# Load order and slots of the expert weights, load order and ends of the modulation slabs in a two-layer decoder trunk

## The chip, the cores and the metric

The kernel runs on one core of one Trainium2 chip, in one launch. The metric is the device time in microseconds (us): the median of the timed runs. Besides them there is one profiled execution, from which every row below is read.

## The reference

One sequence of 512 tokens with 1024 features, float32, goes through two layers. Each layer is a mixer and then a mixture of experts; both are modulated by a vector `c` through `mod = silu(c) @ ada_w + ada_b`, six groups of 1024 columns for each layer.

```python
for layer in range(2):
    sh1, sc1, g1, sh2, sc2, g2 = split(silu(c) @ ada_w[layer] + ada_b[layer], 6)
    h = x * (1 + sc1) + sh1
    y = moba_gla_mixer(h) if layer == 0 else gated_deltanet_mixer(h)
    x = layer_norm(ALPHA * x + g1 * y)
    h = x * (1 + sc2) + sh2
    # every token: 6 of 64 experts, each silu(h @ gate) * (h @ up) @ down, 1024 -> 256 -> 1024, and one shared expert
    x = layer_norm(ALPHA * x + g2 * moe_ffn(h))
```

All weights are float32 and are read once. One expert has three matrices of 1 MiB (gate, up, down); two layers of 64 experts are 384 MiB of the 572 MB that the core moves.

## The kernel before

**The expert loop** (`moe`). The experts are ordered by how many tokens chose them and packed into 38 blocks (`BLOCKS`): 20 blocks hold one expert, 14 hold two and 4 hold four (blocks 8, 16, 26 and 34), so that a block has at most 128 rows of tokens. Iteration b issues on TensorE, whose order is written out by hand here (`manual_schedule`): the down matmuls of block b-1 (`narrow`, L1369), the gate and up matmuls of block b (`widen`, L1336), sums of finished blocks into the residual (`combine`, L1396), transposes of the next block's tokens (`turn`, L1324) and of the hidden values (`turn_back`, L1347). Where block b-1 has one expert, `widen` goes first. A block of four runs its `narrow` in two halves of two experts; the `widen` of the next block stands between them.

**Where weights land.** Gate and up of an expert go into one of five wide buffers in turn (`eslot`: two `w2`, two `parts`, one `wx`). Down goes into a ring of three buffers (`slot`, tag `w`, `NRING`), which all other weight slabs use too. A buffer is taken in turn, so a load waits until the matmuls that read its buffer's last content are over.

**Order of the loads** (`loads`, `fetch`). All weight loads are issued by SyncE's queue (SP), in the order in which the generator `loads` makes them. It alternates one expert's gate and up (`weight_in`) with the down (`weight_out`) of the expert three places earlier (`LAG = 3`). At the end the last three downs go into wide buffers. `fetch` says how far the generator has come when iteration b is written: all loads of blocks up to b + 2, and two more.

**The modulation slabs.** `ada_slabs` makes nine items for each group of 2048 columns: eight loads of 1 MiB, each followed by one multiply-accumulate on VectorE into one buffer `acc` (L254, L256), and an end. The end (`mod_end`, L268, L269) turns `acc` with sixteen TensorE transposes and sums it with four VectorE reductions. Group (0, 0) is done first, in `start`: its end makes `hT`, the modulated and turned input. The other five groups are spread over layer 0: `fill` runs about three items at each weight slab of the mixer and of `out_project`. When the next item is an end and it isn't the first of its call, `fill` stops and leaves it for the next call. After `out_project` a loop runs what is left. Outside the loop of experts the order on each engine is a planner's, by the order of the program and its own costs.

**Around the start.** `start` loads seven slabs, then the first weight slab of the mixer (`first`), then the eighth slab. The end of the group computes, for each of eight k, `hT[0]` on ScalarE (L1749) and, on VectorE, the product in place (L1750) and the remainder `hT[1]` (L1751). `split` (L218, L220) makes the high and low part of a weight slab on ScalarE and VectorE (or GpSimd, L225) into one of two `parts` buffers.

Of the kernel before, what the change touches and what calls it, by code (L numbers as in the profile page):

```python
# [10 lines left out]
F32 = mybir.dt.float32  # L11
# [4 lines left out]
OP = mybir.AluOpType  # L16
PSUM = bass.MemoryType.PSUM

P = 128
D = 1024  # L20
KT = 8
# [5 lines left out]
FE = 256  # L27
# [6 lines left out]
NX = 1  # L34
EARLY = 4
LEAD = 3
LAG = 3
FOLD = 2
LANES = 64
ALPHA = float(4 ** 0.25)  # L40
# [93 lines left out]
class Kernel:  # L134
# [1181 lines left out]
    def turn(self, M, G):  # L1316

        nc = self.nc
        xT = G["xT"] = M["pool"].tile([P, KT, P], F32, tag="xT", name="xT", bufs=2)
        xv = G["xg"].rearrange("p (c k) -> p k c", k=KT)  # L1320
        for g in range(2):
            pt = self.ptile("tr")
            for k in range(4):
                nc.tensor.transpose(pt[:, k * P:(k + 1) * P], xv[:, 4 * g + k, :], self.ident)  # L1324
            nc.scalar.activation(xT[:, 4 * g:4 * g + 4], pt.rearrange("p (k c) -> p k c", k=4), AF.Copy)  # L1325

    def widen(self, M, G):

        nc, xT = self.nc, G["xT"]
        pg = self.ptile("mm")  # L1330
        pv = pg.rearrange("p (j c) -> p j c", j=2)
        h = G["h"] = M["pool"].tile([P, FE], F32, tag="hh", name="hh", bufs=2)
        for g in range(0, len(G["w"]), 2):
            for i in range(KT):
                for a, n, w in G["w"][g:g + 2]:
                    nc.tensor.matmul(pv[a:a + n], xT[:, i, a:a + n], w[0][:, :, i], start=(i == 0), stop=(i == KT - 1))  # L1336
        nc.scalar.activation(h, pg[:, :FE], AF.Silu)  # L1337
        nc.vector.scalar_tensor_tensor(h, h, G["wt"], pg[:, FE:], op0=OP.mult, op1=OP.mult)  # L1338
        yield
# [59 lines left out]
    def eslot(self, M):  # L1399

        k = M["w"] = (M.get("w", -1) + 1) % (NW2 + 2 + NX)
        if k < NW2:
            return self.tab.tile([P, 4096], F32, tag="w2", name="wslot2", bufs=NW2)
        if k < NW2 + 2:
            return self.parts().rearrange("p j c -> p (j c)").bitcast(F32)
        return M["pool"].tile([P, 4096], F32, tag="wx", name="wslot3", bufs=NX)

    def shared(self, hT, wp, ws):

# [61 lines left out]
    def moe(self, l, hT, nxt, pre=None):  # L1471
# [31 lines left out]

        def loads():

            last = []
            for k, b in enumerate(BLOCKS):
                es = [i if i < SINGLE else nc.values_load(
                    M["order"][:, i:i + 1], engines=SPE, min_val=0, max_val=E - 1,
                    skip_runtime_bounds_check_because="the places are a permutation of the experts") for i, _, _ in b]  # L1510
                w = [[] for _ in es]
                W.append([(a, n, x) for (_, a, n), x in zip(b, w)])
                for x, e in zip(w, es):
                    x.append(self.weight_in(l, e, self.eslot(M)))
                    yield
                    last.append((x, e))
                    while len(last) > (0 if k < SINGLE else LAG):
                        x, e = last.pop(0)
                        x.append(self.weight_out(l, e, self.slot()))
                        yield  # L1520
            for x, e in last:
                x.append(self.weight_out(l, e, self.eslot(M)[:, :2048]))
                yield

        load, started, total = loads(), [0], 2 * E

        def fetch(n):

            while started[0] < min(n, total):
                next(load)  # L1530
                started[0] += 1
# [21 lines left out]
        with ExitStack() as es:  # L1553
# [13 lines left out]
            with self.tc.manual_schedule(engines={mybir.EngineType.PE}):  # L1567
                fetch(sum(2 * len(x) for x in BLOCKS[:LEAD]) + 2)
                self.turn(M, G[0])
                for b in range(NB + 1):  # L1570
# [6 lines left out]
                            todo.append(G[b - 1])  # L1577
                    if b < NB:
                        fetch(sum(2 * len(x) for x in BLOCKS[:b + LEAD]) + 2)
                        G[b]["w"], G[b]["one"] = W[b], len(W[b]) == 1  # L1580
                        row.append(self.widen(M, G[b]))
                    if not todo:
# [131 lines left out]
    def start(self, hT, t4):  # L1714
# [20 lines left out]
        def end(acc):  # L1735
            av = acc.rearrange("p (m c k) -> p m k c", m=2, k=KT)
            for g in range(4):
# [9 lines left out]
                for k in range(2 * g, 2 * g + 2):  # L1747
                    x = xT[k // 2][:, k % 2]
                    nc.scalar.activation(hT[0][:, k], x, AF.Identity, scale=md[:, 1, k:k + 1], bias=md[:, 0, k:k + 1])  # L1749
                    nc.vector.tensor_scalar(x, x, md[:, 1, k:k + 1], md[:, 0, k:k + 1], op0=OP.mult, op1=OP.add)  # L1750
                    nc.vector.tensor_sub(hT[1][:, k], x, hT[0][:, k].bitcast(F32))  # L1751

        spare = []
# [8 lines left out]
            return spare.pop()  # L1762

        todo = self.ada_slabs(0, 0, t4, end, slot)
        for f in todo[:-2]:
            f()
        w_in = d["ev_w_in"][0]
        first = self.slab(w_in, 2048, 256)
        todo[-2]()
        todo[-1]()  # L1770
        self.first = {2048: self.split(first)}
        self.first[3072] = self.split(self.slab(w_in, 3072, 16))
# [1 line left out]
    def run(self):  # L1774
# [5 lines left out]
        with ExitStack() as es:  # L1780
# [8 lines left out]
            def fill(n=3):  # L1789

                n, left[0] = n + left[0], 0
                for i in range(n):
                    if not queue:
                        if not todo:
                            return
                        l, g = todo.pop(0)
                        queue.extend(self.ada_slabs(l, g, t4, self.mod_end(l, g)))
                    if i and len(queue) == 1:
                        left[0] = n - i
                        return  # L1800
                    queue.pop(0)()
# [96 lines left out]
```

## Time and profile before

| | us |
|---|---|
| Median of 3 runs (2145.56 to 2153.2) | 2150.31 |
| Profiled execution, its own time | 2150.13 |
| Span of its instructions | 2148.1 |

| Stretch (us from the start of the span) | What runs |
|---|---|
| 0 to 40.4 | group (0, 0) of the modulation, turning of the input |
| 40.4 to 280.3 | mixer of layer 0 |
| 280.3 to 350 | `out_project` of layer 0 |
| 350 to 402.5 | input of the experts, routing, shared expert |
| 402.5 to 1028 | expert loop of layer 0, first to last expert matmul |
| 1389.6 to 1446.1 | `out_project` of layer 1 |
| 1496.2 to 2117.1 | expert loop of layer 1 |

The engines are PE (TensorE), PEld (its weight loads), DVE (VectorE), ACT (ScalarE), POOL (GpSimd) and SP (SyncE). A small letter q after an engine is its sequencer. An arrow in brackets at the end of a row tells for how long the engine was idle before it and what ended that. PEclk is the granted TensorE clock: 1.00 is 2.4 GHz, 0.50 is 1.2 GHz.

### The profile page before, as it was taken

The page shows a single profiled execution, that of the slowest core. Times are in us where ns is not written, and L with a number is a line of the kernel's source. Part 1 is how long each engine was busy: PE and PEld are TensorE (multiplying, and loading weights), DVE is VectorE, ACT ScalarE, POOL GpSimd, SP SyncE. Part 2 cuts the span into 40 slices and gives each one's busy share as a digit, 9 for nine tenths or more (in the row PEclk, how much of TensorE's full clock was granted, in tenths as well). Part 3 has the DMA queues.
Part 4 walks back from the last instruction along what each step waited for, and adds up shares of the span by engine and source line. Part 5 has one row for each costly group of instructions (what it writes and reads, how often), then busy time and mean ns, then how long its engine had stood idle before and what let it go on. Part 6 is the DMA issues. An engine that isn't in the chain of part 4 may idle for free. (4 is left out here: it accounts for less than half of the span.)

```text
span 2148.1 us, 28655 instructions
## 1 busy us (share of the span) xinstructions
PE 1955.6 (91%) x10619; PEld 1193.5 (56%) x10619; DVE 1236.2 (58%) x3169; ACT 508.3 (24%) x969; POOL 441.2 (21%) x313
## 2 busy tenths in 40 slices
PE   4999878999999999999688999999999999998995
PEld 3777778644443443443567877888443444443432
DVE  6666687844444553542778778578453535544436
ACT  3412533111111111111334455523111111111110
POOL 1222234111010110101034445144211010110102
PEclk9999998999999999999899999999999999999997
DMA  7765455998998989988332111128989989989893
GB/s 296 257 240 186 182 199 195 352 330 325 406 349 351 389 316 361 381 325 300 96 118 59 40 60 60 46 99 309 357 335 365 363 327 402 353 317 405 329 348 126
DMA packets 128679, 572.18 MB, mean 266 GB/s; under 512 B 16943, under 2 KB 54255, under 8 KB 72473
## 3 DMA queue, kind: packets, MB, share of 16 engines
q1 hardware_dynamic: 103600, 499.81, 60.1%
q0 software_dynamic: 19632, 55.79, 9.3%
q10 hardware_dynamic: 5304, 14.72, 1.9%
q8 instruction: 85, 1.39, 0.3%
q14 instruction: 58, 0.47, 0.1%
HBM read 550.33 MB, written 34.61 MB: 272 GB/s over the span
## 5 line engine op out<-in xcount | busy, mean ns | idle before, releaser
L1336 PE MATMUL ps_mm<-wslot,xT 128*64 128x512 f32 (+2 forms) x1216 | 404.5, 596 | 1.1 <-ACT xT L1325 0.8
L1369 PE MATMUL ps_mm<-wslot,hT 128*64 128x512 f32 (+2 forms) x1024 | 329.6, 627 | 20.1 <-DMA wslot<-in_moe_w_down_dram 19.9
L1338 DVE SCALAR_TENSOR_TENSOR hh<-hh,t,ps_mm 128x256 f32<-128x256 f32 x76 | 36.5, 480 | 434.5 <-ACT hh L1337 434.5
L1336 PE MATMUL ps_mm<-parts,xT 128*64 128x512 f32 (+2 forms) x832 | 280.0, 595 | 0.7 <-ACT xT L1325 0.4
L1336 PEld LDWEIGHTS ps_mm<-wslot,xT 128*64 128x64 f32 (+2 forms) x1216 | 142.1, 148 | 218.9 <-issue 205.7
L1369 PEld LDWEIGHTS ps_mm<-wslot,hT 128*64 128x64 f32 (+2 forms) x1024 | 105.5, 152 | 225.1 <-issue 197.5
L232 PE MATMUL ps_mm<-parts,hTh 128*128 128x256 f32 x704 | 206.7, 295 | 14.0 <-DVE op L400 6.9
L1294 POOL DMA_INDIRECT xg<-hd,idx x76 | 86.3, 1136 | 615.1 <-PE ps_tr L1396 525.4
L233 PE MATMUL ps_mm<-parts,hTh 128*128 128x256 f32 x704 | 204.0, 291 | 4.9 <-DVE parts L220 4.2
L234 PE MATMUL ps_mm<-parts,hTl 128*128 128x256 f32 x704 | 203.3, 291 | 0.0
L225 POOL TENSOR_TENSOR parts<-wslot,parts 128x512 fp32r<-128x512 f32 (+1 forms) x79 | 140.6, 1807 | 241.9 <-ACT parts L218 241.8
L1397 DVE TENSOR_TENSOR x<-x,ps_tr 128x512 f32<-128x512 f32 x288 | 183.6, 680 | 11.1 <-PE ps_tr L1396 10.4
L1337 ACT ACTIVATE hh<-ps_mm 128x256 f32<-128x256 f32 x76 | 29.2, 384 | 613.7 <-PE ps_mm L1336 613.7
L1376 POOL DMA_INDIRECT acc<-yh,row x40 | 64.8, 1620 | 498.9 <-DVE yh L1375 498.9
L1336 PEld LDWEIGHTS ps_mm<-parts,xT 128*64 128x64 f32 (+2 forms) x832 | 93.7, 144 | 130.5 <-issue 122.9
L1396 PE MATMUL ps_tr<-yh,ohs 128*128 128x512 f32 x288 | 137.4, 477 | 26.1 <-DVEq L1690 14.0
L232 PEld LDWEIGHTS ps_mm<-parts,hTh 128*128 128x128 f32 x704 | 137.3, 195 | 17.7 <-DVE op L400 4.6
L1325 ACT ACTIVATE xT<-ps_tr 128x512 f32<-128x512 f32 x152 | 84.0, 597 | 245.0 <-PE ps_tr L1324 245.0
L233 PEld LDWEIGHTS ps_mm<-parts,hTh 128*128 128x128 f32 x704 | 137.4, 195 | 6.8 <-DVE parts L220 4.8
L234 PEld LDWEIGHTS ps_mm<-parts,hTl 128*128 128x128 f32 x704 | 136.8, 195 | 2.2 <-issue 0.9
L234 PE MATMUL ps_mm<-hTh,parts 128*128 128x512 f32 (+1 forms) x296 | 120.6, 407 | 9.1 <-POOL parts L225 9.1
L232 PE MATMUL ps_mm<-hTh,parts 128*128 128x512 f32 (+1 forms) x296 | 123.7, 418 | 5.1 <-ACT parts L218 2.5
(456 smaller groups left out, 3124.3 us busy)
## 6 DMA issues: line engine op xcount, KB each, us to landing
wslot<-in_moe_w_down_dram SPq DMA_DIRECT2D x128, 1024.0 KB, 10.4
wslot<-in_moe_w_gate_dram SPq DMA_DIRECT2D x76, 1024.0 KB, 8.2
wslot<-in_moe_w_up_dram SPq DMA_DIRECT2D x76, 1024.0 KB, 11.7
parts<-in_moe_w_gate_dram SPq DMA_DIRECT2D x52, 1024.0 KB, 10.3
parts<-in_moe_w_up_dram SPq DMA_DIRECT2D x52, 1024.0 KB, 8.8
wslot<-in_ada_w_dram SPq DMA_DIRECT2D x44, 1024.0 KB, 5.6
wslot<-in_od_w_in_dram SPq DMA_DIRECT2D x16, 1024.0 KB, 6.2
wslot<-in_ev_w_in_dram SPq DMA_DIRECT2D x12, 1024.0 KB, 6.4
```

What stands on the lines that cost most here:

```text
L225: eng.tensor_sub(lo[:, ks], v[:, ks], hi[:, ks].bitcast(F32))
L232: self.nc.tensor.matmul(out, ah, bh, start=(i == 0), stop=False)
L233: self.nc.tensor.matmul(out, ah, bl, start=False, stop=False)
L234: self.nc.tensor.matmul(out, al, bh, start=False, stop=(i == n - 1))
L1294: self.nc.gpsimd.indirect_dma_start(out=xg, out_offset=None, in_=M["hd"], in_offset=bass.IndirectOffsetOnAxis(ap=idx, axis=0), bounds_chec ...
L1325: nc.scalar.activation(xT[:, 4 * g:4 * g + 4], pt.rearrange("p (k c) -> p k c", k=4), AF.Copy)
L1336: nc.tensor.matmul(pv[a:a + n], xT[:, i, a:a + n], w[0][:, :, i], start=(i == 0), stop=(i == KT - 1))
L1338: nc.vector.scalar_tensor_tensor(h, h, G["wt"], pg[:, FE:], op0=OP.mult, op1=OP.mult)
L1369: nc.tensor.matmul(py[a:a + n], hT[:, k, a:a + n], w[1][:, k, 512 * h:512 * h + 512], start=(k == 0), stop=(k == 1))
L1376: nc.gpsimd.indirect_dma_start(out=M["acc"], out_offset=bass.IndirectOffsetOnAxis(ap=G["tok"], axis=0), in_=yf, in_offset=None, bounds_che ...
L1396: nc.tensor.matmul(po, G["oh"][:, t], y[:, cs], start=(i + k == 0), stop=(i == len(Gs) - 1 and k == 1))
L1397: nc.vector.tensor_add(self.x[t][:, cs], self.x[t][:, cs], po)
```

## The change

- `dslot`: down weights go in turn into four buffers, the ring's three and a new one (`wslot4`, 8 KiB for each partition). The last three downs use them too, no longer wide buffers. For its space `xT` and `hh` have one buffer instead of two.
- `loads`: the order is now that of use. For a block b: some downs of block b-1, then all gates and ups of block b, then the rest of the downs of b-1. Of one expert, its down comes behind the gates and ups of the next block; of two, both come ahead; of four, two ahead and two behind.
- `start`: all eight slabs are loaded ahead of `first`. Every second in-place product goes to GpSimd.
- `fill`: an end is left for the next call only while more than one group has not been begun. So the ends of groups (1, 1) and (1, 2) run in the call that has their last slabs: (1, 1) at the last gate slab of the mixer instead of in `out_project`, and (1, 2) at the last slab of `out_project` instead of behind it.

```diff
-        xT = G["xT"] = M["pool"].tile([P, KT, P], F32, tag="xT", name="xT", bufs=2)
+        xT = G["xT"] = M["pool"].tile([P, KT, P], F32, tag="xT", name="xT", bufs=1)
...
-        h = G["h"] = M["pool"].tile([P, FE], F32, tag="hh", name="hh", bufs=2)
+        h = G["h"] = M["pool"].tile([P, FE], F32, tag="hh", name="hh", bufs=1)
...
+    def dslot(self, M):
+
+        k = M["d"] = (M.get("d", -1) + 1) % (self.NRING + 1)
+        if k < self.NRING:
+            return self.slot()
+        return M["pool"].tile([P, 2048], F32, tag="wy", name="wslot4", bufs=1)
...
-            last = []
-            for k, b in enumerate(BLOCKS):
...
-                for x, e in zip(w, es):
-                    x.append(self.weight_in(l, e, self.eslot(M)))
                     yield
-                    last.append((x, e))
-                    while len(last) > (0 if k < SINGLE else LAG):
-                        x, e = last.pop(0)
-                        x.append(self.weight_out(l, e, self.slot()))
-                        yield
-            for x, e in last:
-                x.append(self.weight_out(l, e, self.eslot(M)[:, :2048]))
-                yield
+
+            def down(b, js):
+                for j in js:
+                    W[b][j][2].append(self.weight_out(l, own[b][j], self.dslot(M)))
+                    yield
+
+            for b in range(NB + 1):
+                n = len(BLOCKS[b - 1]) if b > SINGLE else 0
+                first = n if n == 2 else n // 2
+                yield from down(b - 1, range(first))
+                if b < NB:
+                    yield from wide(b)
+                yield from down(b - 1, range(first, n))
+                if b < SINGLE:
+                    yield from down(b, range(1))
...
-                    nc.vector.tensor_scalar(x, x, md[:, 1, k:k + 1], md[:, 0, k:k + 1], op0=OP.mult, op1=OP.add)
+                    eng = nc.gpsimd if k % 2 else nc.vector
+                    eng.tensor_scalar(x, x, md[:, 1, k:k + 1], md[:, 0, k:k + 1], op0=OP.mult, op1=OP.add)
...
-        for f in todo[:-2]:
+        for f in todo[:-1]:
             f()
         w_in = d["ev_w_in"][0]
         first = self.slab(w_in, 2048, 256)
-        todo[-2]()
         todo[-1]()
...
-                    if i and len(queue) == 1:
+                    if i and len(queue) == 1 and len(todo) > 1:
```

## Rows read from the trace of the kernel before

**Rows 1.** Windows by stage: busy us (count) of PE, PEld, DVE, ACT, POOL; PEclk, DMA, GB/s

```profile
280.30:350.00 69.70, 57.69 (x436) 55.83 (x435) 60.21 (x67) 17.34 (x18) 24.71 (x12) 0.90 0.60 212
402.50:1028.00 625.50, 602.19 (x2474) 270.06 (x2474) 288.72 (x850) 81.42 (x152) 71.50 (x60) 0.98 0.92 348
1389.60:1446.10 56.50, 52.23 (x420) 50.76 (x419) 39.33 (x63) 15.69 (x21) 24.42 (x14) 0.97 0.32 113
1496.20:2117.10 620.90, 597.36 (x2474) 269.35 (x2474) 287.88 (x850) 79.76 (x151) 80.47 (x63) 0.99 0.92 349
```

**Rows 2.** Waits of PEld in either expert loop: us in total, times, longest

```profile
PEld ps_mm L1369 <- DMA wslot<-in_moe_w_down_dram: 13.2, 4, 4.5
PEld ps_mm L1369 <- DMA wslot<-in_moe_w_down_dram: 14.0, 4, 5.1
```

**Rows 3.** PE timeline, blocks 33 to 37 of layer 0: start, duration, instructions, idle before

```profile
963.27 3.70 PE L1369 MATMUL ps_mm<-wslot,hT 128*128 128x512 f32 x8
968.13 3.63 PE L1369 MATMUL ps_mm<-wslot,hT 128*32 128x512 f32 x16
971.69 7.13 PE L1336 MATMUL ps_mm<-wslot,xT 128*128 128x512 f32 x16
...
982.81 6.61 PE L1369 MATMUL ps_mm<-wslot,hT 128*32 128x512 f32 x14 [3.01 <-DMA wslot<-in_moe_w_down_dram]
...
996.52 7.09 PE L1336 MATMUL ps_mm<-wslot,xT 128*64 128x512 f32 x32
...
1011.86 7.07 PE L1336 MATMUL ps_mm<-parts,xT 128*64 128x512 f32 x32
```

**Rows 4.** Timeline of SP's queue in the same stretch

```profile
967.00 0.33 SPq L1302 DMA_DIRECT2D wslot<-in_moe_w_down_dram  x1
967.84 0.33 SPq L1302 DMA_DIRECT2D wslot<-in_moe_w_gate_dram  x1
...
971.76 0.33 SPq L1302 DMA_DIRECT2D wslot<-in_moe_w_down_dram  x1
```

**Rows 5.** Windows with a full DMA, and where PEclk fell in the expert loops

```profile
550.00:600.00 50.00, 49.12 (x220) 23.90 (x221) 27.95 (x86) 6.85 (x13) 6.26 (x5) 1.00 1.00 402
...
845.50:852.30 6.80, 5.63 (x13) 1.25 (x14) 0.69 (x1) 0.63 (x1) 0.00 (x0) 0.50 1.01 428
982.10:988.80 6.70, 5.99 (x14) 1.28 (x14) 0.69 (x1) 0.63 (x1) 0.00 (x0) 0.50 1.01 428
1941.20:1944.60 3.40, 3.40 (x12) 0.75 (x8) 0.69 (x1) 0.02 (x1) 0.00 (x0) 0.50 1.00 424
```

**Rows 6.** DMA issues outside the expert loops: count, KB each, median us to landing

```profile
wslot<-in_ada_w_dram SPq DMA_DIRECT2D x44, 1024.0 KB, 5.6
```

**Rows 7.** DVE timeline: the start, and `out_project` of layer 0

```profile
35.73 2.29 DVE L220 TENSOR_TENSOR parts<-wslot,parts 128x2048 fp32r<-128x2048 f32 x1 [3.82 <-ACT parts L218]
37.94 2.35 DVE L256 SCALAR_TENSOR_TENSOR acc<-wslot,cact,acc 128x2048 f32<-128x2048 f32 x1
...
290.38 1.86 DVE L254 TENSOR_SCALAR acc<-wslot,cact 128x2048 f32<-128x2048 f32 x1
...
311.82 0.42 DVE L402 TENSOR_TENSOR x<-x,op 128x256 f32<-128x256 f32 x1
...
313.12 3.87 DVE L402 TENSOR_TENSOR x<-x,op 128x256 f32<-128x256 f32 x1
```

**Rows 8.** Timeline of SP's queue: the start, and `out_project` of layer 0

```profile
19.54 0.67 SPq L206 DMA_DIRECT2D wslot<-in_ev_w_in_dram  x1
21.97 0.34 SPq L252 DMA_DIRECT2D wslot<-in_ada_w_dram  x1
...
292.27 0.38 SPq L206 DMA_DIRECT2D wslot<-in_ev_w_out_dram  x1
```

**Rows 9.** Waits of PE between 280.3 and 402 us

```profile
PE ps_tr L268 <- DVE mod L269: 4.1, 1, 4.1
```

**Rows 10.** Groups of instructions by line: a product with constants on POOL

```profile
L378 POOL TENSOR_SCALAR x<-x 128x1024 f32<-128x1024 f32 x8 | 11.4, 1434 | 19.5 <-DMA x<-in_x_dram 9.4 <-PE ps_mm L234 7.7 <-DVE x L402 1.7
```

More of the change, by code (lines that the diff above doesn't have):

```diff
@@ L36 @@
 LEAD = 3
-LAG = 3
 FOLD = 2
@@ L1504, in loads, with wide @@
         def loads():
-            last = []
-            for k, b in enumerate(BLOCKS):
+            own = []
+            for b in BLOCKS:
+                own.append([])
+                W.append(None)
+            def wide(b):
                 es = [i if i < SINGLE else nc.values_load(
                     M["order"][:, i:i + 1], engines=SPE, min_val=0, max_val=E - 1,
-                    skip_runtime_bounds_check_because="the places are a permutation of the experts") for i, _, _ in b]
-                w = [[] for _ in es]
-                W.append([(a, n, x) for (_, a, n), x in zip(b, w)])
-                for x, e in zip(w, es):
-                    x.append(self.weight_in(l, e, self.eslot(M)))
-                    yield
-                    last.append((x, e))
-                    while len(last) > (0 if k < SINGLE else LAG):
-                        x, e = last.pop(0)
-                        x.append(self.weight_out(l, e, self.slot()))
-                        yield
-            for x, e in last:
-                x.append(self.weight_out(l, e, self.eslot(M)[:, :2048]))
-                yield
+                    skip_runtime_bounds_check_because="the places are a permutation of the experts")
+                    for i, _, _ in BLOCKS[b]]
+                W[b] = []
+                for (_, a, n), e in zip(BLOCKS[b], es):
+                    W[b].append((a, n, [self.weight_in(l, e, self.eslot(M))]))
+                    own[b].append(e)
+                    yield
+            def down(b, js):
[11 more added lines that the diff above has]
+                    yield from down(b, range(1))
         load, started, total = loads(), [0], 2 * E
@@ L1579, in moe @@
                         fetch(sum(2 * len(x) for x in BLOCKS[:b + LEAD]) + 2)
+                    else:
+                        fetch(total)
+                    if b < NB:
                         G[b]["w"], G[b]["one"] = W[b], len(W[b]) == 1
```

## The prediction

> **What bounds the kernel now.** I read the windows by stage first. The two expert loops take 625.5 and 620.9 us of the 2148.1 us span, and in both TensorE is busy for all but 23 us while the DMA is busy for 0.92 of the time at 348 and 349 GB/s [rows 1]. So TensorE sets the time there, with the loads close behind. Next come the waits: four times in either loop the down matmuls wait for a down load, 13.2 and 14.0 us in all [rows 2]. The timeline of one such place shows which: the second half of a block of four. The first half ran undisturbed in 3.63 us; after the next block's `widen`, which ended at 971.69 + 7.13 = 978.82, the second half should have ended some 3.6 us later and ended at 989.42 [rows 3]. Third, the clock. In three of these eight places it falls to 0.50 (1.2 GHz) just after the wait [rows 5]; in the other five, whose waits are shorter, no row shows a fall. Before the loops, `out_project` of layer 0 is the stage to look at, because layer 1 has the same stage without modulation slabs: 69.7 us against 56.5, with TensorE idle for 12.0 us against 4.3 and PEclk 0.90 against 0.97 [rows 1].
>
> **Part 1, the loads of the experts.** What is there to win: 13.2 + 14.0 = 27.2 us of waits, and half of the 5.63 + 5.99 + 3.40 us that TensorE was busy at half clock [rows 2, 5], 7.5 us. Sum 34.7 us. As a cross-check, the place shown lost 989.42 - 978.82 - 3.6 = 7.0 us, of which the rows name a wait of 3.01 and a slow second half of 6.61 [rows 3].
>
> Why the load is late: with three buffers in turn, the fourth down of block 34 takes the buffer of the first. That is free when the first half is over, at 968.13 + 3.63 = 971.76, and at 971.76 SP issues it [rows 3, 4]. Ahead of it in the queue stand the third down, issued at 967.00, and 2 MiB of gate and up, from 967.84 [rows 4]. It is used from 982.81, 11 us after its issue.
>
> What the change does there: with four buffers the third down takes the buffer of block 32, long free; the fourth takes that of block 33, free at 963.27 + 3.70 = 966.97, and both now stand ahead of the next gates. So one load alone is issued at 967.0. A 1 MiB load outside the loops lands in 5.6 us [rows 6]: 972.6, against 978.8 when it is wanted. The spare is 6.2 us: two more loads ahead of it, at 2.6 to 3.0 us (below), would still fit. I count all eight waits gone.
>
> What is late next: behind the fourth down SP stands still until 967.0, where it had been loading for block 36 already. From 967.0 on, 11 loads follow the fourth down before the last gate and up of block 37: four for block 36, three downs, four for block 37. 1 MiB takes 1.049/0.402 = 2.61 us at the best rate shown and 1.049/0.348 = 3.01 at the loop's mean [rows 1, 5]. So they land at 972.6 + 11 x 2.61 = 1001.3 to 972.6 + 11 x 3.01 = 1005.7. Block 37 starts at 1011.86, or 7.0 us sooner without the loss, at 1004.9 [rows 3]: a new wait of 0 to 0.8 us, and up to 3 if the loads bunch. For block 36 four loads give 984.6 against 996.52 - 7.0 = 989.5: no wait. I take 1 us for each layer, 2 in all; ends 0 and 6.
>
> The buffers given up cost nothing, for what stands between: `turn` of the next block and its copy into `xT` come on TensorE behind the `widen` that reads the old one, and `hh` is read by `turn_back` before the next `widen` ends. If that cover were gone, the next `widen` would wait for the two copies in each of the 76 iterations. The slab for layer 1, loaded last on SP at the end of layer 0's loop, now waits for a down of block 36; the last two blocks and the closing sums still run after that, so it stays hidden.
>
> Part 1: 34.7 - 2 = 33 us; ends 27 and 35.
>
> **Part 2, the ends.** The accumulator is one buffer, so the first step of group (1, 2), at 290.38, waits for the end of group (1, 1), which stands in `out_project`; the slab for the second quarter of `out_project` is issued only when that step is over, at 292.27 [rows 7, 8]. With that end run at the last gate slab instead, the steps and the slabs behind them on SP move ahead. If the stage then ran like layer 1's, it would lose 4.3 us of idle time instead of 12.0, and 57.69 x (0.97 - 0.90) = 4.0 us less to the clock: 11.7 us. The end of group (1, 2) made TensorE wait 4.1 us behind the stage [rows 9]; inside it, other matmuls fill that. Together 15.8 us at most. The transposes themselves only change place.
>
> Against it: VectorE was busy for 60.21 of the 69.70 us [rows 1], so a shorter stage is nearly VectorE's. GpSimd's scaling of the slabs stays and holds VectorE up: one sum of 0.42 us took 3.87 [rows 7]. And the steps and reductions that move into the attention stretch stand on VectorE in front of the softmax. I take half, 8 us. Low end: nothing won and one step of 2.35 us [rows 7] in the way, -2; high end 15.
>
> **Part 3, the start.** The last step of the first group stands at 37.94 behind the split of the mixer's first slab, which started at 35.73 after 3.82 us of idle time [rows 7]. The eighth slab now is issued in the place of that slab, at 19.54 instead of 21.97 [rows 8]. Since the split needs ScalarE's half first, the slab in that place had landed before 35.73; so the step starts 37.94 - 35.73 = 2.2 us sooner at least, and 37.94 - (35.73 - 3.82) = 6.0 at most. The weights come one load later, and their split of 2.29 us now falls among the products. I take 4 us; ends 0 and 6.
>
> The four products on GpSimd have no row. The nearest is a product with constants on twice the columns, 1.43 us [rows 10], so 0.72 each. What they free on VectorE I set against what they cost it. Whether they hold VectorE up no row tells for this pair of operations; the row of 3.87 us shows it for another [rows 7].
>
> The Trainium skill's page "SBUF — State Buffer", section "Who interferes with whom", says that a VectorE instruction with two inputs in SBUF is blocked for the whole of a GpSimd instruction that reads SBUF. The trace agrees for the sum of 3.87 us. By it each of four remainders (L1751, two inputs in SBUF) could wait 0.72 us: an estimate of 2.9 us, which would leave 1.1 of the 4 and make the total 2108.
>
> **Sum.** 33 + 8 + 4 = 45 us. The profiled execution took 2150.1 us in all, 2.0 more than its span, and the median is 2150.3: 2150.1 - 45 = 2105. If all low ends came, 27 - 2 + 0 = 25 us: 2125; all high ends, 35 + 15 + 6 = 56: 2094.
>
> **The rivals.**
> 1. *The ends win nothing.* The planner puts the moved transposes where TensorE waits for their last step, or the softmax waits for the steps. For it: VectorE's load. Against it: layer 1 shows the stage at 56.5 us. Time: 2150 - 33 + 2 = 2119.
> 2. *The planner does not keep the new order*, or the fourth buffer comes free too late, and the waits in the blocks of four stay. For it: only TensorE's order is written by hand. Against it: SP's queue follows the program in the place shown [rows 4]. Time: 2150 - 8 - 4 = 2138.
> 3. *Slower: the loops become bound by the loads.* A gate load now stands in SP's one queue behind a down that waits for a `narrow`, as at 967.0, so the DMA runs dry there, and it has little spare. A loop has 192 loads. At 3.26 us for each they last 625.5 us, as long as now; at 3.4 it would be 653 us, two loops 27 + 32 us longer, less 12 from parts 2 and 3: 2198. It decides from 3.26 us. Against it: 2.61 to 3.01 us [rows 1, 5], and the pauses come where loads are ahead.
>
> **How the numbers follow.** The forecast, 2105, gets 0.80, with 2092 to 2122 as its own range; rival 1 0.09, rival 2 0.05, rival 3 0.03, and 0.03 for a result within 0.3%, where small losses eat the gain. 0.3% (6.5 us) is about what a measurement of this kernel can tell from no change. Low 2090, a little past the high ends; high 2128, which takes in rival 1 and the low ends. Outside it lie rivals 2 and 3, the result within 0.3% and the tails. Faster 0.94, same 0.03, slower 0.03.
>
> **What would show it.** Right: the waits of L1369 for down loads gone in both loops, the loops near 607 and 606 us, PEclk never at 0.50 in blocks 26 and 34; `out_project` of layer 0 near 60 us; the first transposes of the modulation's end before 38 us instead of after 40.3. Wrong: waits of L1336 for gate or up loads, above all at block 37; a longer attention stretch before 280 us; matmuls of `out_project` waiting behind L268. The forecast fails most easily in part 2, where the planner decides.

## The result, and the profile after

The changed kernel takes 2095.25 us (median of 4 runs, 2093.2 to 2098.19) against 2151.76 for the kernel before beside it (4 runs, 2145.56 to 2157.92): a ratio of 0.9747, 95% interval 0.9728 to 0.9766, so 54 us less, 50 to 59 by the interval. Here and below a ratio and its interval are the record's estimates over the runs of both kernels; "less" is worked out from them, and the medians alone can differ by another amount (here 56.5 us). The forecast was 2105, range 2090 to 2128. The two profiled spans, 2148.1 and 2091.1 us, differ by 57.0 us, and the stages below add up to that.

| Stretch | before, us | after, us | change |
|---|---|---|---|
| start, up to the first transposes of the end of group (0, 0) | 40.4 | 34.6 | -5.9 |
| from there to `out_project` of layer 0 | 239.9 | 240.6 | +0.7 |
| `out_project` of layer 0 | 69.7 | 62.1 | -7.6 |
| behind it, to the first expert matmul | 52.5 | 46.0 | -6.5 |
| expert loop of layer 0 | 625.5 | 603.7 | -21.8 |
| between the loops | 468.2 | 469.4 | +1.2 |
| expert loop of layer 1 | 620.9 | 603.2 | -17.7 |
| behind it | 31.0 | 31.6 | +0.6 |

Nothing outside the stages that the change touches moved by more than 1.2 us. The windows of the changed kernel that answer [rows 1] follow: length, busy us (count) of PE, PEld, DVE, ACT and POOL, then PEclk, DMA share and GB/s.

```profile
275.10:337.20 62.10, 55.80 (x436) 54.83 (x435) 48.21 (x69) 15.37 (x17) 26.42 (x14) 0.92 0.39 143
337.20:383.20 46.00, 42.23 (x369) 39.94 (x367) 38.35 (x195) 16.87 (x27) 19.00 (x17) 1.00 0.79 295
383.20:986.90 603.70, 590.38 (x2474) 268.32 (x2474) 287.43 (x847) 81.47 (x152) 78.93 (x60) 0.99 0.93 360
1351.60:1407.50 55.90, 51.17 (x416) 50.12 (x416) 39.73 (x61) 14.37 (x15) 25.09 (x14) 0.97 0.31 113
1456.30:2059.50 603.20, 589.79 (x2474) 267.75 (x2474) 287.50 (x850) 79.41 (x151) 80.23 (x63) 0.99 0.93 359
```

In the two loops TensorE is now idle for 13.3 and 13.4 us instead of 23.3 and 23.5, and busy for 11.8 and 7.6 us less with the same 2474 instructions: the rest of the gain is busy time. A matmul that runs at half clock or is starved in the middle of a group counts as busy (the slow second half of [rows 3] stands there as 6.61 us of work), so idle time alone would have shown only half of the gain.

**The loops.** The long waits of the down matmuls [rows 2] are gone. Three groups of the waits of `narrow` for loads that are left in the changed kernel (line, us in total, times, longest) are these: the largest and the one for downs of layer 0, and the one for downs of layer 1:

```profile
PEld ps_mm L1368 <- DMA wslot<-in_moe_w_up_dram: 3.2, 4, 0.8
...
PEld ps_mm L1368 <- DMA wslot<-in_moe_w_down_dram: 0.8, 1, 0.8
...
PEld ps_mm L1368 <- DMA wslot<-in_moe_w_down_dram: 1.5, 2, 0.8
```

None, of these or of the others, is longer than 0.8 us, where [rows 2] had 4.5 and 5.1, and they belong to the weight loads (PEld) alone: no matmul of `narrow` waits for a load. The PE timeline of the place that [rows 3] showed (start, duration, line, instructions):

```profile
929.62 3.70 PE L1368 MATMUL ps_mm<-wslot,hT 128*128 128x512 f32 x8
...
934.49 3.63 PE L1368 MATMUL ps_mm<-wslot,hT 128*32 128x512 f32 x16
938.04 7.13 PE L1335 MATMUL ps_mm<-wslot,xT 128*128 128x512 f32 x16
945.11 3.63 PE L1368 MATMUL ps_mm<-wslot,hT 128*32 128x512 f32 x16
...
955.85 7.09 PE L1335 MATMUL ps_mm<-wslot,xT 128*64 128x512 f32 x32
...
971.19 7.07 PE L1335 MATMUL ps_mm<-parts,xT 128*64 128x512 f32 x32
```

The second half of block 34 (945.11) takes 3.63 us as the first does, right behind the `widen`, and the `widen` of block 37 (971.19) takes 7.07 us, as in [rows 3]: no new wait. SP's queue there, which answers [rows 4]:

```profile
933.36 0.33 SPq L1301 DMA_DIRECT2D wslot<-in_moe_w_down_dram  x1
934.20 0.33 SPq L1301 DMA_DIRECT2D wslot<-in_moe_w_gate_dram  x1
...
951.48 0.33 SPq L1301 DMA_DIRECT2D parts<-in_moe_w_up_dram  x1
```

The fourth down is issued at 933.36, when block 33 is over (929.62 + 3.70 = 933.32), ahead of block 36's gates, and is used 11.75 us later. The prediction had it issued at that very point, with 5.6 us to land and 6.2 to spare.

**`out_project`.** Between the start of this stage and the first expert matmul TensorE waits less for VectorE. In the kernel before it had waited for the product `op` and for the split `parts`:

```profile
PE ps_mm L232 <- DVE op L400: 6.9, 3, 3.6
...
PE ps_mm L233 <- DVE parts L220: 4.1, 2, 2.3
```

In the changed kernel no wait for `parts` is left there, and these two stand at the top, of which the second answers [rows 9] (2.0 us instead of 4.1):

```profile
PE ps_mm L231 <- DVE op L399: 3.0, 1, 3.0
...
PE ps_tr L267 <- DVE mod L268: 2.0, 1, 2.0
```

Three rows of VectorE's timeline around the stage, with one of GpSimd's:

```profile
247.89 1.91 DVE L253 TENSOR_SCALAR acc<-wslot,cact 128x2048 f32<-128x2048 f32 x1
...
293.58 11.17 POOL L385 TENSOR_TENSOR wslot<-wslot,grow 128x2048 f32<-128x2048 f32 x2
...
293.65 6.69 DVE L255 SCALAR_TENSOR_TENSOR acc<-wslot,cact,acc 128x2048 f32<-128x2048 f32 x1 [2.07 <-DMA wslot<-in_ada_w_dram]
...
300.77 4.27 DVE L401 TENSOR_TENSOR x<-x,op 128x256 f32<-128x256 f32 x1
```

The first step of group (1, 2) runs at 247.89, 27 us ahead of the stage, where it stood 10 us inside it [rows 7]. VectorE is still slow while GpSimd scales two slabs, from 293.58 to 304.75: a sum of 0.42 us takes 4.27, a step of 2.35 takes 6.69.

**The start.** Timelines of SP, of VectorE, of PE and of GpSimd in the changed kernel, for [rows 7, 8]:

```profile
19.42 0.36 SPq L251 DMA_DIRECT2D wslot<-in_ada_w_dram  x1
...
32.05 2.35 DVE L255 SCALAR_TENSOR_TENSOR acc<-wslot,cact,acc 128x2048 f32<-128x2048 f32 x1 [0.20 <-DMA wslot<-in_ada_w_dram]
...
34.55 3.65 PE L1764 MATMUL ps_tr<-call,acc 128*128 128x128 f32 x16 [1.40 <-DVE acc L255]
...
43.48 1.30 POOL L1772 TENSOR_SCALAR xT<-xT,md 128x512 f32<-128x512 f32 x1 [3.06 <-DVE xT L1772]
43.53 0.69 DVE L1773 TENSOR_TENSOR hTl<-xT,hTh 128x512 fp32r<-128x512 f32 x1
```

The last step of the first group starts at 32.05 instead of 37.94, 5.9 us sooner, at the upper end of what [rows 7] left open (2.2 to 6.0), and the transposes follow it.

### The profile page after: what moved, and what is told of

Read it like the earlier page. It is cut to its first block, busy times and chain, and to the rows that moved or that the text cites. A ratio compares the mean times of both kernels' runs of the same rounds, so it can differ in the third digit from the quotient of the medians.

```text
span 2091.1 us, 28643 instructions
## 1 busy us (share of the span) xinstructions
PE 1935.5 (93%) x10619; PEld 1189.4 (57%) x10619; DVE 1234.7 (59%) x3165; ACT 507.1 (24%) x969; POOL 453.8 (22%) x317
## 5 line engine op out<-in xcount | busy, mean ns | idle before, releaser
L1368 PE MATMUL ps_mm<-wslot,hT 128*64 128x512 f32 (+2 forms) x1024 | 312.8, 610 | 0.2
L1293 POOL DMA_INDIRECT xg<-hd,idx x76 | 93.5, 1230 | 579.6 <-PE ps_tr L1395 497.0
L255 DVE SCALAR_TENSOR_TENSOR acc<-wslot,cact,acc 128x2048 f32<-128x2048 f32 x38 | 122.7, 3230 | 13.6 <-DMA wslot<-in_ada_w_dram 13.2
L231 PE MATMUL ps_mm<-hTh,parts 128*128 128x512 f32 (+1 forms) x296 | 124.2, 419 | 4.8 <-ACT parts L217 2.5
```

The source lines that it names most:

```text
L231: self.nc.tensor.matmul(out, ah, bh, start=(i == 0), stop=False)
L255: nc.vector.scalar_tensor_tensor(acc, w, self.cact[:, k:k + 1], acc, op0=OP.mult, op1=OP.add)
L1293: self.nc.gpsimd.indirect_dma_start(out=xg, out_offset=None, in_=M["hd"], in_offset=bass.IndirectOffsetOnAxis(ap=idx, axis=0), bounds_chec ...
L1368: nc.tensor.matmul(py[a:a + n], hT[:, k, a:a + n], w[1][:, k, 512 * h:512 * h + 512], start=(k == 0), stop=(k == 1))
```

## The experiments

### Each part alone

**The loads alone**, on the kernel before: `dslot`, `loads`, one buffer for `xT` and `hh`, as in the diff of the change, and a `fetch(total)` in the last iteration.

> The kernel before with part 1 alone: the new order of the loads, the fourth down buffer, one buffer each for xT and hh. Theory (the parts are independent, and each is worth what its own stretch of the changed kernel shows): the two loops take 603.7 and 603.2 us instead of 625.5 and 620.9, so the whole is 39.5 us shorter, about 2111 us; out_project of layer 0 stays at 69.7 and the stretch before it at 280.3. Of the 39.5 us, 35.4 lie in the eight second halves of the blocks of four and should be there in any run; the other 4 are places where the clock fell without a wait ahead of it, and may fall elsewhere. Rival (the sum of the prediction as it stands): 33 us, 2117, with a wait of 1 us for a gate or up load at block 37 of each loop, which only the other parts took away. Rival 2: the parts need each other, and alone this one wins under 25 us.

Measured: 2106.91 us against 2146.37, ratio 0.9809 (0.9789 to 0.983), 41 us less (the medians differ by 39.5). Its loops:

```profile
396.70:1000.80 604.10, 590.78 (x2474) 268.10 (x2474) 288.18 (x850) 81.37 (x152) 71.36 (x60) 0.99 0.93 360
1467.60:2070.50 602.90, 589.56 (x2474) 267.66 (x2474) 287.43 (x850) 79.41 (x151) 80.25 (x63) 0.99 0.93 359
```

They are the loops of the changed kernel to 0.4 us. The part is independent of the others, and no wait stands at block 37 here either. Rival 2 is out; 33 us lies outside the interval (36 to 45).

**The ends alone**, on the kernel before:

```diff
-                    if i and len(queue) == 1:
+                    if i and len(queue) == 1 and len(todo) > 1:
```

> The kernel before with part 2 alone: the condition in fill. Theory: out_project of layer 0 falls from 69.7 to about 62 us and the stretch from its last projection to the first expert matmul from 52.5 to about 46, 14 us together, 2136 us in all. Rival (as predicted, half of what could be won): 8 us, 2142. Rival 2 (rival 1 of the prediction: the ends win nothing, and the shorter stretches come from the earlier start of the stage): within 3 us of 2150. If the moved end delays the softmax, the stretch from 40.4 to 280.3 us grows from 239.9 by 1 to 2 us.

Measured: 2135.7 us, ratio 0.9938 (0.9918 to 0.9958), 9 to 18 us less, 13.3 in the middle (the medians differ by 10.7). From the start of `out_project` to the first expert matmul, the kernel before:

```profile
280.30:402.50 122.20, 103.83 (x818) 99.73 (x816) 102.10 (x270) 34.73 (x45) 44.64 (x28) 0.92 0.64 231
```

and with the ends alone:

```profile
280.90:387.50 106.60, 96.11 (x801) 92.64 (x799) 86.18 (x264) 32.11 (x44) 45.17 (x29) 0.98 0.56 209
```

15.6 us less. Not all of it stays: the stretch ahead of `out_project` carries the moved transposes. From the first transposes of `start` to the stage it took 239.0 to 242.1 us in the seven profiles with that end moved, 240.6 on average, and 234.1 to 239.9 in the seven without, 236.9 on average: some 4 us, more than the 1 to 2 expected. The theory of 14 us lies in the interval and 8 us just outside it; rival 2 is out.

**One end alone**, that of group (1, 1), on the kernel before:

```diff
-                    if i and len(queue) == 1:
+                    if i and len(queue) == 1 and len(todo) != 1:
```

> Half of part 2 on the kernel before: only the end of group (1, 1) runs in the call that has its last slab; that of (1, 2) stays behind out_project. With both moved, the stretch from the start of out_project to the first expert matmul fell from 122.2 to 106.7 us, of which 7.5 were out_project itself and 6.5 to 7 the stretch behind its last projection, and the stretch from the start's end to out_project was 0 to 5 us longer. Theory (the one accumulator is what counts: once (1, 1) is out of the way, the steps of (1, 2) and the slabs behind them run ahead): out_project falls to about 58 us, since the transposes of (1, 2), 4.1 us, are then not in it; behind it remain 52.4; together 110 to 111, so the first end brings some 11.5 us of the stretch and the second 3.5; the whole 8 to 10 us below before. Rival (each end brings what its own stretch shows): out_project 62, behind it 52.4, together 114 to 115; 7.5 and 7; the whole 4 to 6 us below before.

Measured: 2138.83 us against 2148.94, ratio 0.9948 (0.9929 to 0.9968), 11 us less. Its `out_project`, and the stretch behind it:

```profile
282.40:339.70 57.30, 51.92 (x419) 50.77 (x418) 43.21 (x60) 15.06 (x16) 24.91 (x13) 0.97 0.39 146
339.70:390.60 50.90, 45.43 (x383) 43.13 (x381) 41.25 (x203) 17.37 (x27) 18.93 (x16) 0.97 0.71 266
```

108.2 us together: the first end brings 14.0 of the 15.6, and the second 1.6. With both ends moved the same stretch took 106.6 to 108.3 us in the four profiles without extra copies (108.1 in the changed kernel's), so what the second end wins isn't clear of the scatter. Once the steps of (1, 2) run ahead of it, the stage takes 57.3 us, close to layer 1's 55.9. The theory holds, with more for the first end than the 11.5 us expected, and the rival falls; the second end mostly moves its work from behind the stage into it.

**The start alone**, on the kernel before: the loads of `start` and the products on GpSimd, as in the diff of the change.

> The kernel before with part 3 alone: the eighth slab ahead of the mixer's first, every second product on GpSimd. Theory: the transposes of the end start at 34.6 us instead of 40.4, out_project 5 us sooner, and nothing behind it gives that back: 2145 us, 5 less. Rival (as predicted): 4 us, 2146. Rival 2: the later weights and the products on GpSimd take it back before 280 us, and the whole is within 1.5 us of 2150.

Measured: 2141.48 us, ratio 0.9969 (0.9954 to 0.9985), 3 to 10 us less, 6.7 in the middle (the medians differ by 4.9). The transposes start at 34.9, `out_project` at 272.7. Theory and rival both lie in the interval; rival 2 does not.

**The order of the slabs without GpSimd**, on the kernel before:

```diff
-        for f in todo[:-2]:
+        for f in todo[:-1]:
             f()
...
-        todo[-2]()
```

> Part 3 with the new order of the slabs alone, all eight products on VectorE, on the kernel before. In the changed kernel the four products on GpSimd took 1.25 to 1.74 us each, where 0.72 was estimated, and the remainders on VectorE kept 0.68 to 0.69 us. Theory: the products on GpSimd neither win nor lose: the same time as with them, within 1 us (2145), with VectorE 2.2 us busier (four times 0.54) and two waits for GpSimd, 0.51 and 0.59 us, gone. Rival (GpSimd holds VectorE up, as the page weighed in the prediction has it): without them 2 to 3 us less, 2142. Rival 2: they free VectorE where it counts: 1 to 2 us more, 2147.

Measured: 2144.67 us, ratio 0.9988 (0.9972 to 1.0004), not clear of no change, though its transposes start at 34.6 too. That reads as if GpSimd were worth 3 us. So the question was put once more, on the changed kernel:

```diff
-                    eng = nc.gpsimd if k % 2 else nc.vector
-                    eng.tensor_scalar(x, x, md[:, 1, k:k + 1], md[:, 0, k:k + 1], op0=OP.mult, op1=OP.add)
+                    nc.vector.tensor_scalar(x, x, md[:, 1, k:k + 1], md[:, 0, k:k + 1], op0=OP.mult, op1=OP.add)
```

> The changed kernel with all eight in-place products of the start on VectorE. On the kernel before, the order of the slabs won 2.7 us without the products on GpSimd and 5.7 with them (means of 12 and 9 runs, 1.3 us of uncertainty on the difference). Theory (the products on GpSimd free VectorE where it counts): 2 to 4 us more than the changed kernel beside it. Rival (they neither win nor lose, and that difference was chance): within 1.5 us. Rival 2 (GpSimd's reads hold VectorE up): 2 to 3 us less.

> The changed kernel once more, beside the one with all products on VectorE. Theory: 0.9747 of before, as it was; loops within 1.5 us of 603.7 and 603.2, and no wait at block 37 in this run either. The sum of the parts measured alone is 41.0 + 13.3 + 6.7 = 61 us, 54 to 57 were measured for the whole: if they are only additive within their scatter, this run stays at 53 to 58.

Measured: 2088.77 us without GpSimd, ratio 0.9732 (0.9708 to 0.9756), and 2094.61 with it, ratio 0.9744 (0.9721 to 0.9767). The sign has turned: by the means it is 3 us for GpSimd on the kernel before and 3 us against it here, and the intervals overlap both times. What the four products on GpSimd are worth stays open, its sign too. The changed kernel itself came out as before, with loops of 603.3 and 603.3 us.

### Which half of part 1 does it

**The order without the fourth buffer**, on the kernel before: `loads`, `fetch(total)`, single `xT` and `hh`, and, in the new `loads`,

```diff
-                    W[b][j][2].append(self.weight_out(l, own[b][j], self.dslot(M)))
+                    W[b][j][2].append(self.weight_out(l, own[b][j], self.slot()))
```

> Part 1 with the new order of the loads, but the downs in the ring's three buffers only (xT and hh single, as in part 1). By the prediction's reckoning at block 34: the fourth down still waits for the first half, so it is issued at 971.76, but now with nothing ahead of it, and lands 5.6 us later, at 977.4, when it is wanted at 978.8. So theory A (the order is enough for the downs): the eight waits of the narrow matmuls go here too, and the price comes behind them, because SP stands still 4.8 us longer: 11 loads at 2.61 to 3.01 us end at 1006.1 to 1010.5 where block 37 wants the last at 1004.9, a wait for gate or up of 1.2 to 5.6 us in each loop, possibly behind the other blocks of four too. Loops 605 to 612 us, the whole 25 to 37 us below before. Theory B (the slot is what counts): the narrow matmuls keep most of their 27 us of waits, and the loops stay above 618 us.

Measured: 2111.89 us against 2152.17, ratio 0.9813 (0.9797 to 0.9829), 40 us less. The windows of its loops:

```profile
401.60:1007.10 605.50, 592.01 (x2474) 268.81 (x2474) 288.23 (x850) 81.50 (x152) 71.50 (x60) 0.99 0.93 359
1475.90:2083.10 607.20, 593.32 (x2474) 269.99 (x2474) 287.50 (x850) 79.74 (x151) 80.31 (x63) 0.99 0.92 357
```

and the PE timeline of layer 0 around blocks 34 and 37:

```profile
953.46 3.63 PE L1369 MATMUL ps_mm<-wslot,hT 128*32 128x512 f32 x16
...
964.08 3.63 PE L1369 MATMUL ps_mm<-wslot,hT 128*32 128x512 f32 x16
...
990.17 1.02 PE L1336 MATMUL ps_mm<-parts,xT 128*64 128x512 f32 x2
991.36 7.08 PE L1336 MATMUL ps_mm<-parts,xT 128*64 128x512 f32 x30 [0.17 <-DMA parts<-in_moe_w_up_dram]
```

Theory A holds. The fourth down can't be issued before 953.46 + 3.63 = 957.1, and is there at 964.08, 7.0 us later; in the kernel before, the matmuls wanted it just as long after its issue (971.76 to 978.8) and waited. Seven of the eight second halves take 3.63 to 3.85 us; that of block 26 in layer 1 still takes 5.03. The price stands at block 37: its `widen` takes 991.36 + 7.08 - 990.17 = 8.27 us instead of 7.07, so 1.2 us, the low end of what was expected, and in layer 1 no such wait is longer than 0.4 us. The whole, 37 to 44 us by the interval, lies at the upper end of the 25 to 37 expected or above it.

**The fourth buffer without the order**, on the kernel before: `dslot` and single `xT` and `hh`, and

```diff
-                        x.append(self.weight_out(l, e, self.slot()))
+                        x.append(self.weight_out(l, e, self.dslot(M)))
```

> Part 1 with the fourth down buffer alone, in the old order of the loads (down three experts behind, the last three in wide buffers; xT and hh single). With four buffers the third down of block 34 goes where the last one of block 32 was, free since 938, so SP doesn't stand still before 967.0, when the fourth down takes the buffer of block 33; ahead of it are at most the gate and up of one expert, 2 MiB, 5.2 to 6.0 us. Theory A (the slot is enough): the fourth down is there by 967.0 + 6.0 + 5.6 = 978.6 at the latest, wanted at 978.8: waits of the narrow matmuls under 3 us in each loop instead of 13 to 14, loops at 603 to 608 us, the whole 30 to 41 us below before. Theory B (the order is needed: the gates ahead of the fourth down make it late): waits of 1 to 4 us stay behind each block of four, loops at 612 to 620 us.

Measured: 2108.02 us, ratio 0.9795 (0.9779 to 0.9811), 44 us less; the loops take 605.1 and 602.8 us. SP's queue and the second half of block 34:

```profile
943.43 0.33 SPq L1302 DMA_DIRECT2D wslot<-in_moe_w_up_dram  x1
949.79 0.33 SPq L1302 DMA_DIRECT2D wslot<-in_moe_w_down_dram  x1
...
961.55 3.73 PE L1369 MATMUL ps_mm<-wslot,hT 128*32 128x512 f32 x16
```

Theory A holds here too. The fourth down is issued at 949.79 and has 11.8 us until it is used, 4.8 more than in the kernel before, and the load ahead of it was issued 6.4 us sooner, at 943.43. Either half of part 1 does what both do together, within the intervals. In block 34 the wait of [rows 3, 4] needed two things at once: a late issue, and 2 MiB of gate and up issued just ahead of it. Taking away either one is enough.

**One buffer for `xT` and `hh`**, on the kernel before: the two lines `bufs=1` of the diff.

> The kernel before with one buffer for xT and hh, nothing else. Theory (the prediction's: the turn of the next block comes behind the widen that reads the old xT, and hh is read before it is written again): the loops stay at 625.5 and 620.9 us, each within 3 us (the clock falls in other places from run to run), with no new wait of the widen matmuls for xT or of the activation for hh. Rival (the cover has a hole): a wait of 0.3 to 0.6 us in each of the 76 iterations, 11 to 23 us for each loop.

Measured: 2147.48 us, in one run. Its loops:

```profile
398.00:1023.40 625.40, 602.01 (x2474) 270.08 (x2474) 288.72 (x850) 81.35 (x152) 71.55 (x60) 0.98 0.92 348
1491.60:2113.20 621.60, 598.34 (x2474) 269.13 (x2474) 287.79 (x850) 79.64 (x151) 80.17 (x63) 0.99 0.92 348
```

They stand at 625.4 and 621.6 us against 625.5 and 620.9, and the waits of `widen` for `xT` are no longer than before (0.5 us at most): the cover that the prediction named holds.

### From where the loads would bind

**More traffic**, on the changed kernel: in every block SP also copies rows of a down matrix to a DRAM tile that nobody reads.

```diff
+            M["more"] = self.tc.dram_tile([NB * 192, D], F32, name=f"more{l}")
...
                         fetch(sum(2 * len(x) for x in BLOCKS[:b + LEAD]) + 2)
+                        r = (64, 192)[l]
+                        nc.sync.dma_start(M["more"][b * r:(b + 1) * r], self.d["moe_w_down"][l][b][:r])
```

> The changed kernel with more traffic on the same queue and engines, whose result nobody reads: in every block of the loops a copy from DRAM to DRAM of rows of a down matrix, 256 KiB in layer 0 (5% more bytes) and 768 KiB in layer 1 (15% more). It asks from which point the loads set the time (rival 3). The changed loops take 603.7 and 603.2 us at a DMA share of 0.93, so at a full share their 192 MiB would last 561 us, 2.92 us for each. Theory (TensorE sets the time until the share reaches 1): layer 0 stays within 3 us of 603.7 (561 x 1.05 = 589), layer 1 becomes bound by the loads, 561 x 1.15 = 645 us, with waits of the widen matmuls for gates and ups of some 40 us. Rival (the queue's pauses behind the blocks of four bind earlier): layer 0 already grows by 5 to 15 us. Rival 2 (copies cost less than loads): layer 1 stays under 625.

This asked nothing of the loops (one run, 2142.06 us). They took 606.1 and 603.3 us at a DMA share of 0.94 and 0.93, as without copies, because the planner issued the copies where SP was free. They came out elsewhere: from the start of `out_project` to the first expert matmul it took 125.8 us instead of 108.1, and between the loops 499.2 instead of 469.4. There TensorE starved, as the window behind the first loop shows:

```profile
1006.30:1065.00 58.70, 15.84 (x55) 11.76 (x56) 26.92 (x46) 7.82 (x11) 3.26 (x6) 0.53 0.84 285
```

So the second try also took SP's order from the program:

```diff
-            with self.tc.manual_schedule(engines={mybir.EngineType.PE}):
+            with self.tc.manual_schedule(engines={mybir.EngineType.PE, mybir.EngineType.SP}):
```

> The extra copies again (256 KiB in each block of layer 0, 768 KiB in layer 1; nobody reads them). In the first try the planner moved them out of the loops to where the queue was free, so the loops had no more traffic than before. Here SP's order in the loops is that of the program, as TensorE's is, and a copy stands behind the loads of each block. The loads of the changed loops take 603.7 and 603.2 us at a DMA share of 0.93, so at a full share 561 us. Theory (TensorE sets the time until the share is near 1): layer 0, 5% more bytes, 589 us of transfers, stays within 4 us of 603.7; layer 1, 15% more, 645 us of transfers, becomes bound by them at 640 to 650 us, with some 40 us of waits of the widen or narrow matmuls for loads. Rival (the queue's pauses behind the blocks of four bind earlier, rival 3 of the prediction with a lower threshold): layer 0 already grows by 5 to 20 us. Rival 2: copies cost the queue less than loads, layer 1 stays under 625.

Measured: 2128.73 us, in one run. The windows of its loops:

```profile
384.70:987.90 603.20, 589.92 (x2474) 267.97 (x2474) 287.02 (x847) 81.47 (x152) 78.84 (x60) 0.99 0.97 377
1454.50:2092.70 638.20, 605.87 (x2474) 272.89 (x2474) 285.17 (x846) 79.36 (x151) 78.54 (x60) 0.98 0.98 386
```

and the longest waits of TensorE in that of layer 1:

```profile
PE ps_mm L1335 <- DMA parts<-in_moe_w_up_dram: 10.5, 2, 5.9
...
PE ps_mm L1335 <- DMA wslot<-in_moe_w_up_dram: 6.0, 1, 6.0
```

5% more bytes cost nothing, at a share of 0.97. 15% more cost 35 us, a little less than the theory's 640 to 650 us for the loop, with `widen` waiting for ups. The bound loop moved 192 + 28.5 = 220.5 MiB in 638.2 us, 2.89 us for each. The loop at 603.2 us has 3.14 us for each of its 192, so by this estimate, which counts a copied MiB like a loaded one, it has about 8% to spare.

## Why the prediction was right, term by term

The mechanism of each part was right, and the total of 45 us fell 12 short of the 57.0 in the spans, 9 short of the 54 by the ratio. Parts 1 and 2 were sized too small; for part 3 the timed runs don't tell 4 us from 6. Part 1 passed its own high end of 35 us, and the whole came out next to 2094, where all the high ends were summed: the range held because its low end went past them.

**Part 1: 33 predicted, 39.5 measured** (625.5 - 603.7 and 620.9 - 603.2). What was to be won, 34.7, was won: all eight second halves run undisturbed. In the timelines of TensorE they took 64.7 us together before and 29.0 after, so 35.7. Two terms were off. (The low end of 27 isn't the sum of its own terms either: 34.7 - 6 is 28.7.)
- The new wait at block 37, taken as 2 us in all, isn't there. The 11 loads were counted at 2.61 to 3.01 us, and the lower price had given no wait. The first row below shows the changed kernel's DMA in that stretch:

```profile
945.00:971.00 26.00, 24.92 (x109) 11.19 (x110) 12.11 (x23) 4.80 (x9) 1.56 (x1) 1.00 1.01 425
...
869.60:873.00 3.40, 3.40 (x15) 2.14 (x15) 1.12 (x8) 2.15 (x4) 1.09 (x1) 0.52 1.02 369
```

 At 425 GB/s 1 MiB takes 2.47 us. From 933.36 + 5.6 = 938.96, 11 loads at that price end at 966.1, an estimate, 5 us before block 37 starts. The mean of a loop was a poor upper price, since it also holds the pauses of the queue. The wait does exist, 1.2 us of it in layer 0, where the queue stands still for longer: in the run with the order alone.
- Falls of the clock that no wait explains weren't in the sum. In the kernel before:

```profile
743.50:766.90 23.40, 22.57 (x106) 11.55 (x105) 13.00 (x46) 2.99 (x6) 2.60 (x2) 1.00 0.89 357
...
766.90:770.30 3.40, 3.40 (x8) 0.79 (x9) 1.50 (x6) 0.00 (x0) 1.10 (x1) 0.51 1.03 348
1859.20:1862.60 3.40, 3.40 (x6) 0.86 (x7) 1.76 (x12) 0.00 (x0) 1.10 (x1) 0.51 1.03 365
1995.70:1999.10 3.40, 3.40 (x17) 2.71 (x16) 1.52 (x10) 2.34 (x4) 1.04 (x1) 0.51 1.03 364
```

 Three such places, behind the `widen` of the blocks 22 and 30, are not in the changed kernel's loops: half of 3 x 3.40 us, 5.1 us. A fourth stays, at 869.60 in the changed kernel (the second row of the fence above). In block 4 the clock falls in both loops of every profile; in this pair it stays down for 6.8 us in layer 1 after the change, from 1518.2, and for 3.4 before, from 1558.9, which takes 1.7 back. 35.7 + 5.1 - 1.7 = 39.1 of the 39.5 measured. In part this is luck of the pair, in part it isn't: outside the blocks 4, 8, 16, 26 and 34 the six profiles with the old loads have 2 to 5 such falls, 3.3 on average, and the six with part 1 or one half of it and no copies 0 to 2, 1.2 on average. Counted at half of 3.4 us each, the difference is worth 3.6 us in a typical run. Why there are fewer isn't settled.

**Part 2: 8 predicted, 11 to 13 measured** (alone 13.3 us by the ratio and 10.7 by the medians; 15.6 less 4 by stages). Halving the ceiling of 15.8 was wrong, and the ceiling came nearly true in another way than it was made up. The first end was counted at 11.7 us and brought 14.0, of which 12.4 lie in the stage itself; the second was counted at 4.1, because "inside it, other matmuls fill that", and brought 1.6, not clear of the scatter: inside the stage TensorE still waits 2.0 us for the end's last step, and the stage is 62.1 us with that end in it and 57.3 without. VectorE's load was named as what would hold the stage; its 60.21 us fell to 48.21, because the steps run ahead of the stage, and 14 of its 62.1 us are now free of VectorE, where 9.5 of 69.7 were. The other counter-argument, the stretch ahead, did bite, with about 4 us. The prediction had priced it in the low end alone, with one step of 2.35 us; whether it is the steps on VectorE, which is busy for 176.35 us there instead of 157.95, or the moved transposes, no run separates.

**Part 3: 4 predicted, 5.9 measured at the transposes**; alone 3 to 10 us by the timed runs, so that these would fit 4 as well. In the trace the upper end of the bracket came true, because the step now starts when its slab has landed (idle for 0.20 us until then) and waits for no split. How much of it lasts to the end of the kernel is less sure: with the same 5.9 us the order of the slabs without GpSimd won between -1 and 6.

By the Trainium skill's page "SBUF — State Buffer", section "Who interferes with whom", the prediction had estimated 2.9 us against this part: four remainders, each blocked by a product on GpSimd. The rows don't agree for this pair: the remainder at 43.53 took its usual 0.69 us while a product ran on GpSimd from 43.48, and it is the product that was long, 1.30 us where [rows 10] scale to 0.72. The same page of the Trainium skill makes it depend on who issues first which of the two is blocked, a condition that the prediction left out. Here GpSimd's row starts first, by 0.05 us, and yet it was not VectorE that lost time.

**The rivals.** Rival 1 (the ends win nothing) fell with the two runs on the ends. Rival 2 (the planner does not keep the order) fell with the timeline: SP kept the order of the program. Yet its fear, that the planner moves loads, came true for the copies that nothing depends on. Rival 3 (the loads bind) was to decide from 3.26 us for each load; a loop that is really bound takes 2.89, and the faster loops still leave 3.14.

**Do the parts add?** Alone they give 1.91, 0.62 and 0.31%, 2.84 together, against 2.53 for the whole (2.34 to 2.72); each has an interval of about 0.2 either way. By the medians it is 39.5 + 10.7 + 4.9 = 55.1 us against 56.5. In the stages of the two profiles they add: 39.5 + (7.6 + 6.5 - 0.7) + 5.9 = 58.8, less the 1.8 us by which the untouched stretches grew. No sign is left that one part needs another.

## What to carry to other kernels

A wait for a load has two sides, when it is issued and what is in flight ahead of it. Look at both before a buffer is spent: here a new order of the loads alone did what a fourth buffer alone did. Cost a wait with its busy side too, since half of the gain was in matmuls that ran starved or at half clock and counted as busy. And a single accumulator orders everything that goes through it: ending one group earlier was worth 14 us in the stage and the stretch behind it, of which the stretch ahead gave some 4 back, although that end has the same sixteen transposes as before.

## What the runs showed of the hardware

- The granted clock fell to 0.51, about its lower level of 1.2 GHz, at 766.90 us in the kernel before, while TensorE was busy for the whole 3.4 us; in the stretch ahead, from 743.50, it had been busy for 22.57 of 23.40 us at full clock. So not every fall needs a wait for a load ahead of it.
- The DMA kept 425 GB/s at a share of 1.01 for 26 us beside matmuls that were busy for 24.92 us, and 5% more traffic in a loop cost no time.
- A product with constants on GpSimd over 512 columns took 1.25 to 1.74 us beside VectorE's work, against 0.54 on VectorE (one of four there took 0.92). Halving the row for 1024 columns gave 0.72.
- A load that the matmuls wanted 7.0 us after its issue came too late with 2 MiB of other loads issued just ahead of it, in the kernel before, and in time without them, in the run with the order alone.
